# GpSimd's elementwise work put on VectorE, gather buffers lent to query reads, and two heads routed singly in a two-layer hybrid kernel

## The chip, the core and the metric

The kernel runs on one core of a Trainium2 chip. The core has a matrix engine (TensorE, PE in the profile), a vector engine (VectorE, DVE), an activation engine (ScalarE, ACT), a general engine (GpSimd, POOL) and a sequencer that only issues transfers (SyncE, SP). Each works through its own list of instructions in order; semaphores tie the lists together. The metric is the device time of one execution in microseconds (us).

## What is computed

Two layers over 256 tokens of width 1024, all in float32. The first half of a layer (called the mixer here) is an attention of 8 heads, a short convolution and two gates; the second half (the expert stage) is a product-key expert layer. Cut to what matters:

```
ada = c @ w_ada[l] + b_ada[l]                    # shift, scale, gate of both halves
h = rmsnorm(x) * (1 + sc1) + sh1
proj = h @ w_in[l]                               # q, k, v, conv and gate columns
x = x + g1 * (merged(attention, conv, gates) @ w_out[l])
h = rmsnorm(x) * (1 + sc2) + sh2
q = (h @ w_query[l]).reshape(T, 8, 2, 128)
scores = einsum("thpd,hpnd->thpn", q, sub_keys)  # 128 keys in each half of a head
top 16 of each half -> 256 sums -> top 16        # 16 experts of 16384 in each head
a = gelu(einsum("td,thkd->thk", h, expert_u[idx]))
x = x + g2 * einsum("thk,thkd->td", softmax(best) * a, expert_v[idx])
```

## The kernel before

**Mixer.** Weights come from HBM in groups of two 128x1024 tiles (1 MB), in the fixed order of a list called `stream`. `load_ahead` issues them on SP's queue as soon as one of three `raw` buffers is free. `next_unit` takes the next tile. A weight tile is split into two parts for the matmuls: ScalarE copies it to `wh` (L340), and then `wl = raw - wh` is formed (L345). Which engine forms `wl` is chosen by `l_engine`: a running sum grows by `pol["pool"]` with each tile, and a tile goes to GpSimd whenever the sum reaches one. The shares are the constants `POOL_START`, `POOL_MIX` and `POOL_PROJ` (L39), and 1.0 near the end of a mixer and of a layer. Between the weight groups lie groups of `w_ada`, which VectorE reduces: L288 multiplies a tile by the broadcast vector `cbc` and sums it up, L285 adds a scaled tile to a row. The low parts of the normalized input, `hl`, are formed at L536 and L624, partly on GpSimd.

**Query and routing.** For 16 column blocks `n`, TensorE forms queries (L940) and scores (L924). The two token tiles are `t = 1` and `t = 0`. `route` finds, for two heads of a tile at once (four key lists, `nh` is not yet a parameter), the best 16 of each list, the best 16 sums and the experts' numbers: it is a generator whose pieces `fill` places in VectorE's program between other work, up to a budget in each step.

**Experts.** Tile 0 is done densely: all 128 blocks of `expert_u` (the U stretch, L1099) and of `expert_v` (the V stretch, L1157) pass TensorE, 64 groups of 1 MB each, weighed by products of one-hot matrices that `onehots` makes (L1068 on VectorE, L1069 on GpSimd, L1071 on ScalarE). Tile 1 is done by gathers: GpSimd issues an indirect transfer for each of 128 slots (L991), 512 KB each, from `expert_u` and again from `expert_v`, into eight buffers `rows`, two in each of four `pairs`; VectorE takes them one by one (L1007, L1015) in `use`, after which the buffer goes to the next gather. `issue` issues gathers as long as a buffer is free and the heads concerned are routed.

**Lent memory.** Some tiles of the expert stage have no use yet when its reads begin, and are lent to the query and U reads: eight parts of the two activation tiles (`al`, `ah` in the profile), `hot`, and the four pairs. `place` numbers the groups of a layer: the 8 query groups are -8 to -1, the U groups 0 to 63. A lent part carries the last place for which it may be used, and `spare_part` gives a read the first part that still allows its place. Before the change all four pairs carry -5, so only one read (place -5) goes to a pair; the gathers own the pairs from the first issue on.

Of the kernel before, what the change touches and what calls it, by code (L numbers as in the profile page):

```python
# [37 lines left out]

POOL_START, POOL_MIX, POOL_PROJ = 0.5, (0.6, 0.4), 0.34  # L39


def f(ap):
    return ap.bitcast(F32)
# [3 lines left out]
def body(ctx: ExitStack, tc: tile.TileContext, d: dict, out: bass.AP):  # L47
# [469 lines left out]
    def first_norm(xps):  # L517
# [13 lines left out]
        def shift(k):  # L531
            a, b = acol[:, 0, 0, k:k + 1], adac[:, 0, 0, k:k + 1]
            z = work.tile([128, S], F32, name="hf", bufs=4)
            A.activation(hh[:, k], xh[:, k], AF.Identity, bias=b, scale=a)
            A.activation(z, xh[:, k], AF.Identity, bias=b, scale=a)
            (V if k == KD - 1 else G).tensor_tensor(hl[:, k], z, f(hh[:, k]), op=OP.subtract)  # L536

# [46 lines left out]
    def norm(l, w, kind, xps):  # L584
# [34 lines left out]
        for k in range(KD):  # L619
            while len(zs) < LEAD and k + len(zs) < KD:  # L620
                zs.append(shift(k + len(zs)))
            z, b = zs.popleft()
            if k % 2:
                G.tensor_tensor(hl[:, k], z, f(hh[:, k]), op=OP.subtract)  # L624
            else:
                V.scalar_tensor_tensor(hl[:, k], z, b, f(hh[:, k]), op0=OP.add, op1=OP.subtract)
            products(k, False)
            if k:
                products(k - 1, True)
# [19 lines left out]
    def mixer(pool, l, hh, hl, pss, vp=None):  # L649
# [157 lines left out]
        for k in range(KD - 2):  # L807
# [5 lines left out]
            tick()  # L813
        pol["pool"] = 1.0
        more["pool"] = None
# [11 lines left out]

    def route(pool, t, q, s4, sel, l, idx, whole):


        tv = pool.tile([128, 4, 16], F32, name="tv", bufs=2)
        ti = pool.tile([128, 4, 16], U32, name="ti", bufs=2)
        for i in range(4):
            while i == 2 and not whole():
                yield None
            s = s4[:, i]
            V.max(tv[:, i, 0:8], s)
            V.max_index(ti[:, i, 0:8], tv[:, i, 0:8], s)
            V.match_replace(s, tv[:, i, 0:8], s, LOW)
            V.max(tv[:, i, 8:16], s)  # L840
            V.max_index(ti[:, i, 8:16], tv[:, i, 8:16], s)
            yield 1700
        tf = pool.tile([128, 4, 16], BF, name="tf", bufs=2)
        V.tensor_copy(tf, ti)
        cand = s4.rearrange("p (n q) (a b) -> p n (q a) b", q=2, b=16)
        tvt = tv.rearrange("p (h q) k -> p h q k", q=2)
        V.tensor_tensor(cand, tvt[:, :, 0, :, None].to_broadcast([128, 2, 16, 16]),
                        tvt[:, :, 1, None, :].to_broadcast([128, 2, 16, 16]), op=OP.add)
        yield 1100
        bv = pool.tile([128, 2, 16], F32, name="bv", bufs=2)  # L850
        bp = pool.tile([128, 2, 16], U32, name="bp", bufs=2)
        for n in range(2):
            s = cand[:, n].rearrange("p a b -> p (a b)")
            V.max(bv[:, n, 0:8], s)
            V.max_index(bp[:, n, 0:8], bv[:, n, 0:8], s)
            V.match_replace(s, bv[:, n, 0:8], s, LOW)
            V.max(bv[:, n, 8:16], s)
            V.max_index(bp[:, n, 8:16], bv[:, n, 8:16], s)
            yield 2300

        cols = slice(32 * q, 32 * q + 32)
        g = sel[:, 2, cols].rearrange("p (n k) -> p n k", n=2)
        V.tensor_tensor(g, bv, bv[:, :, 0:1].to_broadcast([128, 2, 16]), op=OP.subtract)
        after(2, lambda: A.activation(g, g, AF.Exp))
        pos = pool.tile([128, 2, 32], U32, name="pos", bufs=2)
        bpf = bp.rearrange("p n k -> p (n k)")
        V.tensor_scalar(pos[:, 0], bpf, 4, None, op0=OP.logical_shift_right)
        V.tensor_scalar(pos[:, 1], bpf, 15, None, op0=OP.bitwise_and)
        posf = pool.tile([128, 2, 32], BF, name="posf", bufs=2)
        V.tensor_copy(posf, pos)  # L870
        yield 800
        tft = tf.rearrange("p (h q) k -> p h q k", q=2)
        for x in range(2):
            oh = pool.tile([128, 2, 16, 16], BF, name="oh")
            pf = posf[:, x].rearrange("p (n k) -> p n k", n=2)
            V.tensor_tensor(oh, pf[:, :, :, None].to_broadcast([128, 2, 16, 16]),
                            io16[:, None, None, :].to_broadcast([128, 2, 16, 16]), op=OP.is_equal)
            V.tensor_tensor(oh, oh, tft[:, :, x, None, :].to_broadcast([128, 2, 16, 16]), op=OP.mult)
            V.tensor_reduce(sel[:, x, cols].rearrange("p (n k) -> p n k", n=2), oh, axis=AX.X, op=OP.add)
            yield 1900  # L880
        if idx is not None:
            e = pool.tile([128, 32], F32, name="ei", bufs=2)
            V.tensor_scalar(e, sel[:, 0, cols], 128.0, float(l * 128 * NE), op0=OP.mult, op1=OP.add)
            V.tensor_tensor(e, e, sel[:, 1, cols], op=OP.add)
            V.tensor_copy(idx[:, cols], e)
            yield 400
# [69 lines left out]
    def experts(es, xp, rp, low, halves, pairs, hot, l, hf, pss):  # L956
# [69 lines left out]
        def route_all():  # L1026
            for t in (1, 0):
                for q in range(4):
                    while (t, q) not in scores:
                        yield None  # L1030
                    yield from route(rp, t, q, scores[t, q], sel[t], l, idx if t else None,
                                     lambda: (t, q) in whole)
                    if t:
                        routed.add(q)
            for _ in range(3):
# [13 lines left out]
        def step(n):  # L1049
            fill(3600 if n < 9 else 2400)  # L1050
            issue()
            if n >= 9:
                use()

        bg.append(route_all())
        query(l, hf, pss, rp, got, step)
        issue()


        def onehots(half, b):  # L1060
# [73 lines left out]
        for e in range(0, NE, 2):  # L1134
# [54 lines left out]
    for l in range(DEPTH):  # L1189
# [95 lines left out]
```

## Time and profile before

| | us |
|---|---|
| three runs, median (lowest to highest) | 1861.13 (1859.49 to 1862.21) |
| the profiled execution, its own time | 1862.17 |
| its span in the trace | 1860.4 |
| TensorE busy | 1608.0 |
| VectorE busy | 1398.7 |
| GpSimd busy | 945.4 |
| ScalarE busy | 575.4 |

The transfers moved 669.24 MB, 360 GB/s over the span. In the profile's 40 slices the rate stands between 178 and 341 GB/s in the two mixers, and between 391 and 416 GB/s in nearly all the rest. The page shows no wait of its own for the mixers: they have to be read as stretches, 0 to 248 us and 925 to 1154 us. The query block columns follow each (248 to 325, 1154 to 1232), then the U and the V stretch.

### The profile page before, as it was taken

The page shows a single profiled execution, that of the slowest core. Times are in us where ns is not written, and L with a number is a line of the kernel's source. Part 1 is how long each engine was busy: PE and PEld are TensorE (multiplying, and loading weights), DVE is VectorE, ACT ScalarE, POOL GpSimd, SP SyncE. Part 2 cuts the span into 40 slices and gives each one's busy share as a digit, 9 for nine tenths or more (in the row PEclk, how much of TensorE's full clock was granted, in tenths as well). Part 3 has the DMA queues.
Part 4 walks back from the last instruction along what each step waited for, and adds up shares of the span by engine and source line. Part 5 has one row for each costly group of instructions (what it writes and reads, how often), then busy time and mean ns, then how long its engine had stood idle before and what let it go on. Part 6 is the DMA issues. An engine that isn't in the chain of part 4 may idle for free.

```text
span 1860.4 us, 26229 instructions
## 1 busy us (share of the span) xinstructions
PE 1608.0 (86%) x9527; PEld 1260.9 (68%) x9527; DVE 1398.7 (75%) x2681; ACT 575.4 (31%) x1257; POOL 945.4 (51%) x731
## 2 busy tenths in 40 slices
PE   6799989986789989887789999998786998898776
PEld 4788878986789644532357997898785994444222
DVE  7797859999988767654565877699997887666455
ACT  3464332111166433300046443221113653431001
POOL 3435204444589777755341231244446987776551
PEclk7899999988989999999999999999898999999998
DMA  8668788999999999999945677899999999999996
GB/s 318 249 227 298 295 341 298 408 409 409 408 391 395 411 415 415 415 415 415 397 178 199 252 291 263 328 377 408 409 408 394 392 404 416 414 415 412 416 416 271
DMA packets 163203, 669.24 MB, mean 360 GB/s; under 512 B 16001, under 2 KB 16001, under 8 KB 146690
## 3 DMA queue, kind: packets, MB, share of 16 engines
q1 hardware_dynamic: 87346, 396.39, 54.3%
q0 software_dynamic: 73856, 268.48, 36.4%
q10 hardware_dynamic: 1872, 2.69, 0.4%
q8 instruction: 75, 1.23, 0.3%
q14 instruction: 54, 0.44, 0.1%
HBM read 666.46 MB, written 1.05 MB: 359 GB/s over the span
## 4 chain that ended last, share of the span: by engine, by line
DVE 31%; DMA 27%; PE 24%; issue 8%; POOL 6%; ACT 3%; SPq 0%; POOLq 0%; DVEq 0%; ACTq 0%
DMA rows<-in_expert_v_dram,idx 15%; PE mm L1099 8%; DVE rows L1007 7%; DMA raw<-in_expert_v_dram 6%; PE yp L1157 4%; POOL rows L991 4%; PE wp L1086 3%; DVE raw L288 3%; DVE y L1015 3%; DMA rows<-in_expert_rows_dram,idx 2%; DVE wl L345 2%; PE mm L394 2%; PE mm L395 1%; PE mm L396 1%; ACT wh L340 1%
## 5 line engine op out<-in xcount | busy, mean ns | idle before, releaser
L991 POOL DMA_INDIRECT rows<-in_expert_rows_dram,idx x256 | 305.6, 1194 | 335.4 <-DVE rows L1007 90.4
L991 POOL DMA_INDIRECT rows<-in_expert_v_dram,idx x256 | 329.9, 1289 | 234.2 <-DMA rows<-in_expert_v_dram,idx 97.5
L1015 DVE SCALAR_TENSOR_TENSOR y<-rows,cv,y 128x1024 f32<-128x1024 f32 x254 | 335.1, 1319 | 146.8 <-DMA rows<-in_expert_v_dram,idx 140.4
L1007 DVE SCALAR_TENSOR_TENSOR rows<-rows,h 128x1024 f32<-128x1024 f32 x256 | 328.7, 1302 | 0.4 <-DMA rows<-in_expert_rows_dram,idx 0.3
L1157 PE MATMUL yp<-raw,ah 128*128 128x512 f32 x512 | 238.9, 613 | 60.6 <-DMA raw<-in_expert_v_dram 59.4
L345 POOL TENSOR_TENSOR wl<-raw,wh 128x1024 fp32r<-128x1024 f32 x52 | 136.1, 2622 | 267.0 <-ACT wh L340 255.4
L1157 PE MATMUL yp<-raw,al 128*128 128x512 f32 x512 | 241.1, 614 | 33.8 <-DMA raw<-in_expert_v_dram 33.0
L1099 PE MATMUL mm<-hfull,raw 128*128 128x128 f32 x1984 | 239.9, 280 | 20.0 <-ACT al L1113 16.8
L1099 PEld LDWEIGHTS mm<-hfull,raw 128*128 128x128 f32 x1984 | 231.1, 195 | 20.9 <-ACT al L1113 17.2
L1071 ACT ACTIVATE hot<-iotf,iT 128x128 f32<-128x128 f32 x512 | 163.2, 390 | 263.3 <-PE wp L1086 217.5
L1157 PEld LDWEIGHTS yp<-raw,ah 128*128 128x128 f32 x512 | 94.7, 193 | 203.2 <-DMA raw<-in_expert_v_dram 103.9
L1099 PE MATMUL mm<-hfull,ah 128*128 128x128 f32 x1600 | 192.8, 282 | 13.5 <-ACT al L1113 13.5
L1099 PEld LDWEIGHTS mm<-hfull,ah 128*128 128x128 f32 x1600 | 189.3, 199 | 13.8 <-ACT al L1113 13.8
L1157 PEld LDWEIGHTS yp<-raw,al 128*128 128x128 f32 x512 | 93.8, 193 | 138.0 <-issue 96.0
L394 PE MATMUL mm<-hh,wh 128*128 128x256 f32 x512 | 149.8, 293 | 12.3 <-ACT qT L658 6.8
L340 ACT ACTIVATE wh<-raw 128x1024 fp32r<-128x1024 f32 x112 | 116.0, 1052 | 115.9 <-DMA raw<-in_w_gt_dram 47.9
L1086 PEld LDWEIGHTS wp<-hot 128*128 128x128 f32 x1024 | 129.1, 192 | 31.9 <-issue 28.5
L1069 POOL TENSOR_TENSOR hot<-hot,gT 128x256 f32<-128x256 f32 x128 | 148.6, 1161 | 2.3
L395 PE MATMUL mm<-hl,wh 128*128 128x256 f32 x512 | 146.3, 286 | 0.0
L396 PE MATMUL mm<-hh,wl 128*128 128x256 f32 x512 | 146.1, 285 | 0.0
L1086 PE MATMUL wp<-hot 128*128 128x64 f32 x1024 | 128.3, 268 | 2.8 <-POOL hot L1069 2.8
L345 DVE TENSOR_TENSOR wl<-raw,wh 128x1024 fp32r<-128x1024 f32 x60 | 92.4, 1548 | 45.4 <-ACT wh L340 45.3
(230 smaller groups left out, 2346.4 us busy)
## 6 DMA issues: line engine op xcount, KB each, us to landing
raw<-in_expert_v_dram SPq DMA_DIRECT2D x128, 1024.0 KB
raw<-in_expert_u_dram SPq DMA_DIRECT2D x62, 1024.0 KB
ah<-in_expert_u_dram SPq DMA_DIRECT2D x50, 1024.0 KB
raw<-in_w_adat_dram SPq DMA_DIRECT2D x64, 512.0 KB
raw<-in_w_gt_dram SPq DMA_DIRECT2D x16, 1024.0 KB
raw<-in_w_adag_dram SPq DMA_DIRECT2D x16, 1024.0 KB
raw<-in_w_cv_dram SPq DMA_DIRECT2D x12, 1024.0 KB
raw<-in_w_qk_dram SPq DMA_DIRECT2D x8, 1024.0 KB
```

Source lines behind the costliest of these rows:

```text
L345: l_engine().tensor_tensor(lo, raw, f(h), op=OP.subtract)
L394: T.matmul(ps, h[:, c], mh[:, k], start=first, stop=False)
L395: T.matmul(ps, h[:, c], ml[:, k], start=False, stop=False)
L396: T.matmul(ps, lo[:, c], mh[:, k], start=False, stop=last)
L991: G.indirect_dma_start(out=t, out_offset=None, in_=rows[kind], in_offset=bass.IndirectOffsetOnAxis(ap=idx[:, s:s + 1], axis=0))
L1007: V.scalar_tensor_tensor(t, t, 1.0, h1, op0=OP.mult, op1=OP.mult, accum_out=av[:, s:s + 1])
L1015: V.scalar_tensor_tensor(y1, t, cv[:, s:s + 1], y1, op0=OP.mult, op1=OP.add)
L1069: G.tensor_tensor(q, q, gT[:, ts, None].to_broadcast([128, TB, 64]), op=OP.mult)
L1071: A.activation(p[:, i], iotf, AF.Abs, bias=iT[:, b * TB + i:b * TB + i + 1])
L1086: T.matmul(ps[:, t], p[:, t], q[:, t], start=True, stop=True)
L1099: T.matmul(ps[:, u + x], raw[:, x, k * 128:(k + 1) * 128], hf[:, k, :128], start=(k == 0), stop=(k == KD - 1))
L1157: T.matmul(ys[q], halves[i // 64][:, i % 64], raw[:, x, q * 512:(q + 1) * 512], start=(i == 0), stop=(i == NE - 1))
```

## The change

Three parts. First, every elementwise instruction that GpSimd had, except three at the very end of the kernel, goes to VectorE: `wl`, `hl`, and the product in `onehots`. GpSimd keeps the gathers. Second, the four pairs carry the last places -5, -4, -3 and -2, so that they take four query reads; `free` starts empty, and `release`, called at each query step, hands a pair to the gathers once the read that was in it has been used and no later read may take it. Third, for tile 1 the first two heads are routed one after the other, each on half the lists, and `issue` looks at the head and not at the pair of heads.

```
-POOL_START, POOL_MIX, POOL_PROJ = 0.5, (0.6, 0.4), 0.34
+POOL_START, POOL_MIX, POOL_PROJ = 0.0, (0.0, 0.0), 0.0
...
-            (V if k == KD - 1 else G).tensor_tensor(hl[:, k], z, f(hh[:, k]), op=OP.subtract)
+            V.tensor_tensor(hl[:, k], z, f(hh[:, k]), op=OP.subtract)
...
-        pol["pool"] = 1.0
+        pol["pool"] = 0.0
...
-    def route(pool, t, q, s4, sel, l, idx, whole):
+    def route(pool, h0, nh, s4, sel, l, idx, whole):
...
-        for i in range(4):
+        for i in range(2 * nh):
...
-        free = deque(pair[:, i] for i in range(2) for pair in pairs)
+        free = deque()
+
+        def release():
+
+            for p in list(pairs):
+                if any(t is p for _, t in spare_of.values()):
+                    continue
+                here = [x for x in spare if x[1] is p]
+                if here:
+                    if place.get(state["dma"], 0) <= here[0][0]:
+                        continue
+                    spare.remove(here[0])
+                pairs.remove(p)
+                free.extend(p[:, i] for i in range(2))
...
-            while tasks and free and tasks[0][1] in routed:
-                assert not any(last < 0 for last, _ in spare_of.values())
+            while tasks and free and (tasks[0][1], tasks[0][2] // 16) in routed:
...
+                    for h in range(2) if t and q == 0 else [None]:
...
+                        yield from route(rp, 2 * q + (h or 0), 2 if h is None else 1, s4, sel[t], l,
+                                         idx if t else None, lambda: (t, q) in whole)
...
             fill(3600 if n < 9 else 2400)
+            release()
             issue()
...
-            G.tensor_tensor(q, q, gT[:, ts, None].to_broadcast([128, TB, 64]), op=OP.mult)
+            V.tensor_tensor(q, q, gT[:, ts, None].to_broadcast([128, TB, 64]), op=OP.mult)
...
-        for t in pairs:
-            give_back((-5, t))
+        for i, t in enumerate(pairs):
+            give_back((-5 + i, t))
```

Three places in the instruction lists show it. On VectorE, in the first layer's first norm (`wl` is the low part of a weight tile, `hl` that of the input, `raw` the tile itself):

```order
 L345 TENSOR_TENSOR wl_194<-raw_101,wh_193 128x1024
+L536 TENSOR_TENSOR hl<-hf,hh 128x256
+L345 TENSOR_TENSOR wl_205<-raw_101,wh_204 128x1024
 L345 TENSOR_TENSOR wl_215<-raw_103,wh_214 128x1024
+L345 TENSOR_TENSOR wl_222<-raw_103,wh_221 128x1024
 L288 SCALAR_TENSOR_TENSOR raw_105,adac<-raw_105,cbc 128x1024 x2
 L292 TENSOR_TENSOR adac<-adac,bcol 128x2
 L293 SCALAR_TENSOR_TENSOR acol<-adac,ngc 128x1
+L536 TENSOR_TENSOR hl<-hf,hh 128x256
```

Both halves of a weight group now stand in VectorE's list, between the reductions of `w_ada`. On SP, at the reads for the first layer's query stretch (`rows` are the pairs, `al`, `hot` and `ah` the other lent tiles):

```order
 L198 DMA raw<-in_w_query_dram 128x2x1024 x3
 L198 DMA rows_2296<-in_w_query_dram 128x2x1024
-L198 DMA al<-in_w_query_dram 128x2x1024 x4
-L198 DMA hot<-in_expert_u_dram 128x2x1024
-L198 DMA ah<-in_expert_u_dram 128x2x1024 x4
-L198 DMA raw<-in_expert_u_dram 128x2x1024 x3
+L198 DMA rows_2297<-in_w_query_dram 128x2x1024
+L198 DMA rows_2298<-in_w_query_dram 128x2x1024
+L198 DMA rows_2299<-in_w_query_dram 128x2x1024
+L198 DMA al<-in_w_query_dram 128x2x1024
 L198 DMA al<-in_expert_u_dram 128x2x1024 x3
 L198 DMA hot<-in_expert_u_dram 128x2x1024
```

Three query reads moved from `al` to the pairs, and three U reads took their place in `al`. On GpSimd, the first gathers of the changed kernel (`rows0` to `rows3` are the pairs, two buffers each):

```order
L1004 DMA rows0_2296<-in_expert_rows_dram,idx_2380 128x1024 x2
L1004 DMA rows1_2297<-in_expert_rows_dram,idx_2380 128x1024 x2
L1004 DMA rows0_2296<-in_expert_rows_dram,idx_2380 128x1024 x2
L1004 DMA rows2_2298<-in_expert_rows_dram,idx_2380 128x1024 x2
L1004 DMA rows1_2297<-in_expert_rows_dram,idx_2380 128x1024 x2
L1004 DMA rows3_2299<-in_expert_rows_dram,idx_2380 128x1024 x2
```

Before, the first eight gathers went to the four pairs in turn, twice over; now the third pair enters after six gathers and the fourth after ten.

## Rows read from the trace of the kernel before

**Rows 1.** Stretches: us, busy by engine (x instructions), PE clock, DMA share, GB/s

```profile
0.00:248.00 248.00, 208.32 (x1341) 182.35 (x1341) 198.85 (x266) 109.22 (x201) 92.57 (x53) 0.92 0.73 274
248.00:325.00 77.00, 74.61 (x413) 65.95 (x412) 56.73 (x198) 19.50 (x48) 19.35 (x18) 1.00 0.89 338
525.00:625.00 100.00, 100.00 (x898) 100.00 (x897) 84.75 (x134) 59.47 (x154) 88.99 (x71) 1.00 1.01 395
625.00:925.00 300.00, 252.68 (x748) 122.01 (x746) 183.41 (x284) 64.13 (x166) 185.78 (x148) 0.99 1.02 415
925.00:1154.00 229.00, 211.51 (x1381) 181.28 (x1382) 162.46 (x201) 105.44 (x194) 64.60 (x35) 0.96 0.63 233
```

**Rows 2.** Chain that ended last, 0 to 248 us, then 925 to 1154: shares

```profile
by line: DVE raw L288 21.2%; issue 8.3%; DVE wl L345 6.6%; ACT wh L340 5.6%; DMA raw<-in_w_cv_dram 5.0%; DMA raw<-in_w_gt_dram 4.8%; POOL wl L345 4.7%; DVE acc L285 3.9%; DMA raw<-in_w_cp_dram 2.5%; DMA raw<-in_w_out_dram 2.0%; DMA raw<-in_
...
by line: PE mm L394 10.8%; PE mm L395 9.9%; PE mm L396 9.8%; issue 6.7%; DVE wl L345 6.2%; DMA raw<-in_w_qk_dram 5.6%; ACT wh L340 4.4%; PE yp L1157 4.2%; DMA raw<-in_w_gt_dram 4.2%; DMA raw<-in_expert_v_dram 3.0%; DMA raw<-in_w_adag_dram 2
```

**Rows 3.** Lines by form, 0 to 248 us: count | busy us, mean ns | idle before

```profile
L288 DVE SCALAR_TENSOR_TENSOR raw<-raw,cbc 128x1024 f32<-128x1024 f32 x48 | 82.0, 1745 | 2.9 <-issue 1.6 <-DMA raw<-in_w_adat_dram 1.3
L345 DVE TENSOR_TENSOR wl<-raw,wh 128x1024 fp32r<-128x1024 f32 x27 | 38.3, 1422 | 20.3 <-ACT wh L340 20.2
...
L345 POOL TENSOR_TENSOR wl<-raw,wh 128x1024 fp32r<-128x1024 f32 x29 | 78.6, 2716 | 113.1 <-ACT wh L340 109.7 <-issue 3.4
```

**Rows 4.** Source lines, whole run: duration ns min/median/max, first and last start

```profile
L288 DVE SCALAR_TENSOR_TENSOR raw<-raw,cbc x64: 1210/1219/3425, 10.4 to 1060.7; 128x1024 f32<-128x1024 f32 x64
L345 DVE TENSOR_TENSOR wl<-raw,wh x60: 1207/1224/5683, 16.0 to 1144.2; 128x1024 fp32r<-128x1024 f32 x60
L1068 DVE TENSOR_TENSOR hot<-iotf,jT x128: 409/418/837, 520.5 to 1694.2; 128x256 f32<-128x256 f32 x128
```

**Rows 5.** Timeline: start us, us; a reduction on VectorE beside a subtraction on GpSimd

```profile
62.57 3.42 DVE L288 SCALAR_TENSOR_TENSOR raw<-raw,cbc 128x1024 f32<-128x1024 f32 x1
...
62.47 2.43 POOL L345 TENSOR_TENSOR wl<-raw,wh 128x1024 fp32r<-128x1024 f32 x1 [3.37 <-issue]
```

**Rows 6.** Lines by form, 925 to 1154 us; then timeline at 949 us

```profile
L345 DVE TENSOR_TENSOR wl<-raw,wh 128x1024 fp32r<-128x1024 f32 x33 | 54.1, 1652 | 25.1 <-ACT wh L340 25.1
L345 POOL TENSOR_TENSOR wl<-raw,wh 128x1024 fp32r<-128x1024 f32 x23 | 57.4, 2503 | 153.9 <-ACT wh L340 145.8 <-DVE acc L285 5.9 <-PE mm L396 2.2
...
949.50 2.26 DVE L489 SCALAR_TENSOR_TENSOR ss<-ss 128x2 f32<-128x2 f32 x1
```

**Rows 7.** Timeline of SP's queue, 247 to 335 us

```profile
247.08 0.37 SPq L198 DMA_DIRECT2D rows<-in_w_query_dram  x1
...
260.16 16.19 SPq L198 DMA_DIRECT2D raw<-in_expert_u_dram  x3
302.39 13.79 SPq L198 DMA_DIRECT2D al<-in_expert_u_dram  x3
320.63 0.37 SPq L198 DMA_DIRECT2D hot<-in_expert_u_dram  x1
324.21 11.09 SPq L198 DMA_DIRECT2D ah<-in_expert_u_dram  x4
```

**Rows 8.** Timeline: GpSimd's first gather, VectorE's first use, TensorE's query block 7

```profile
288.05 1.01 POOL L991 DMA_INDIRECT rows<-in_expert_rows_dram,idx  x1 [49.69 <-DVE sc L839]
...
293.79 1.21 DVE L1007 SCALAR_TENSOR_TENSOR rows<-rows,h 128x1024 f32<-128x1024 f32 x1
...
280.13 3.62 PE L940 MATMUL mm<-hfull,rows 128*128 128x256 f32 x16
```

**Rows 9.** Timeline of GpSimd and of VectorE in the U stretch

```profile
529.74 1.78 POOL L991 DMA_INDIRECT rows<-in_expert_rows_dram,idx  x1 [0.16 <-issue]
531.83 0.94 POOL L991 DMA_INDIRECT rows<-in_expert_rows_dram,idx  x1 [0.30 <-issue]
532.79 1.56 POOL L1069 TENSOR_TENSOR hot<-hot,gT 128x256 f32<-128x256 f32 x1
...
534.99 1.57 DVE L1007 SCALAR_TENSOR_TENSOR rows<-rows,h 128x1024 f32<-128x1024 f32 x1
```

More of the change, by code (lines that the diff above doesn't have):

```diff
@@ L623, in norm @@
             if k % 2:
-                G.tensor_tensor(hl[:, k], z, f(hh[:, k]), op=OP.subtract)
+                V.tensor_tensor(hl[:, k], z, f(hh[:, k]), op=OP.subtract)
             else:
@@ L825, in across @@
                 T.matmul(ys[2 * t + q], sl[:, ts], h[:, c], start=False, stop=last)
-    def route(pool, t, q, s4, sel, l, idx, whole):
-        tv = pool.tile([128, 4, 16], F32, name="tv", bufs=2)
-        ti = pool.tile([128, 4, 16], U32, name="ti", bufs=2)
-        for i in range(4):
+    def route(pool, h0, nh, s4, sel, l, idx, whole):
+        tv = pool.tile([128, 4, 16], F32, name="tv", bufs=2)[:, :2 * nh]
+        ti = pool.tile([128, 4, 16], U32, name="ti", bufs=2)[:, :2 * nh]
+        for i in range(2 * nh):
             while i == 2 and not whole():
@@ L842, in route @@
             yield 1700
-        tf = pool.tile([128, 4, 16], BF, name="tf", bufs=2)
+        tf = pool.tile([128, 4, 16], BF, name="tf", bufs=2)[:, :2 * nh]
         V.tensor_copy(tf, ti)
@@ L846, in route @@
         tvt = tv.rearrange("p (h q) k -> p h q k", q=2)
-        V.tensor_tensor(cand, tvt[:, :, 0, :, None].to_broadcast([128, 2, 16, 16]),
-                        tvt[:, :, 1, None, :].to_broadcast([128, 2, 16, 16]), op=OP.add)
+        V.tensor_tensor(cand, tvt[:, :, 0, :, None].to_broadcast([128, nh, 16, 16]),
+                        tvt[:, :, 1, None, :].to_broadcast([128, nh, 16, 16]), op=OP.add)
         yield 1100
-        bv = pool.tile([128, 2, 16], F32, name="bv", bufs=2)
-        bp = pool.tile([128, 2, 16], U32, name="bp", bufs=2)
-        for n in range(2):
+        bv = pool.tile([128, 2, 16], F32, name="bv", bufs=2)[:, :nh]
+        bp = pool.tile([128, 2, 16], U32, name="bp", bufs=2)[:, :nh]
+        for n in range(nh):
             s = cand[:, n].rearrange("p a b -> p (a b)")
@@ L859, in route @@
             yield 2300
-        cols = slice(32 * q, 32 * q + 32)
-        g = sel[:, 2, cols].rearrange("p (n k) -> p n k", n=2)
-        V.tensor_tensor(g, bv, bv[:, :, 0:1].to_broadcast([128, 2, 16]), op=OP.subtract)
+        cols = slice(16 * h0, 16 * h0 + 16 * nh)
+        g = sel[:, 2, cols].rearrange("p (n k) -> p n k", n=nh)
+        V.tensor_tensor(g, bv, bv[:, :, 0:1].to_broadcast([128, nh, 16]), op=OP.subtract)
         after(2, lambda: A.activation(g, g, AF.Exp))
-        pos = pool.tile([128, 2, 32], U32, name="pos", bufs=2)
+        pos = pool.tile([128, 2, 32], U32, name="pos", bufs=2)[:, :, :16 * nh]
         bpf = bp.rearrange("p n k -> p (n k)")
@@ L868, in route @@
         V.tensor_scalar(pos[:, 1], bpf, 15, None, op0=OP.bitwise_and)
-        posf = pool.tile([128, 2, 32], BF, name="posf", bufs=2)
+        posf = pool.tile([128, 2, 32], BF, name="posf", bufs=2)[:, :, :16 * nh]
         V.tensor_copy(posf, pos)
@@ L873, in route @@
         for x in range(2):
[L874 to L879, printed above, removed]
+            oh = pool.tile([128, 2, 16, 16], BF, name="oh")[:, :nh]
+            pf = posf[:, x].rearrange("p (n k) -> p n k", n=nh)
+            V.tensor_tensor(oh, pf[:, :, :, None].to_broadcast([128, nh, 16, 16]),
+                            io16[:, None, None, :].to_broadcast([128, nh, 16, 16]), op=OP.is_equal)
+            V.tensor_tensor(oh, oh, tft[:, :, x, None, :].to_broadcast([128, nh, 16, 16]), op=OP.mult)
+            V.tensor_reduce(sel[:, x, cols].rearrange("p (n k) -> p n k", n=nh), oh, axis=AX.X, op=OP.add)
             yield 1900
         if idx is not None:
-            e = pool.tile([128, 32], F32, name="ei", bufs=2)
+            e = pool.tile([128, 32], F32, name="ei", bufs=2)[:, :16 * nh]
             V.tensor_scalar(e, sel[:, 0, cols], 128.0, float(l * 128 * NE), op0=OP.mult, op1=OP.add)
@@ L1030, in route_all @@
                         yield None
[L1031 to L1034, printed above, removed]
+                    for h in range(2) if t and q == 0 else [None]:
+                        s4 = scores[t, q]
+                        if h == 1:
+                            while (t, q) not in whole:
+                                yield None
+                        s4 = s4 if h is None else s4[:, 2 * h:2 * h + 2]
+                        yield from route(rp, 2 * q + (h or 0), 2 if h is None else 1, s4, sel[t], l,
+                                         idx if t else None, lambda: (t, q) in whole)
+                        if t:
+                            routed.update([(q, 0), (q, 1)] if h is None else [(q, h)])
             for _ in range(3):
@@ L1056, in experts @@
         query(l, hf, pss, rp, got, step)
+        release()
+        assert not pairs
         issue()
@@ L1170, in experts @@
                 finish_block(1, 0)
-        pol["pool"] = 1.0
+        pol["pool"] = 0.0
         finish_block(0, 0)
```

## The prediction

> **What bounds the kernel now.** I read the profile from the outside in. First the stretches [rows 1]: in the V stretch (625 to 925 us) the transfers run at 415 GB/s, with a DMA share of 1.02. I take that as full. In the U stretch (525 to 625 us) TensorE is busy 100.00 of 100 us and the transfers still reach 395 GB/s. So these parts of the expert stage end when their bytes have arrived, or when TensorE is through. In the mixers neither holds: the first (0 to 248 us) moves 274 GB/s, the second (925 to 1154 us) 233 GB/s. Those are the stretches where an engine's order can be worth time. Between them lies the query stretch, 248 to 325 us, at 338 GB/s: against 415 a hole of (415 - 338) x 77 us = 5.9 MB, or 14 us in each layer, is open there.
>
> Next the chain of waits inside the two mixers [rows 2]. In the first, VectorE's reductions (L288) alone are 21.2% of the chain, its subtractions `wl` 6.6%, GpSimd's `wl` 4.7%, while transfers hold 5.0, 4.8, 2.5 and 2.0% and ScalarE's copies 5.6%. In the second mixer TensorE's three matmul lines hold 10.8 + 9.9 + 9.8 = 30.5%, and VectorE's `wl` 6.2%; TensorE is busy there 211.5 of 229 us.
>
> Last the durations. A reduction L288 takes 1219 ns in the median but 1745 ns on average in the first mixer, a `wl` on VectorE 1224 ns in the median and 1422 on average [rows 3, 4]. The timeline says why [rows 5]: at 62.47 us GpSimd starts a `wl` of 2.43 us, at 62.57 us VectorE starts a reduction, and it is through only after 3.42 us, 1.1 us after GpSimd's end. VectorE stood still until GpSimd was done. So GpSimd's help costs VectorE nearly what it saves it.
>
> **Part 1: the subtractions, first mixer.** Sums are made against the profiled execution's own 1862.17 us, 1.0 us above the median of the three runs. Removed: 48 x (1745 - 1219) ns = 25.2 us of standing still at L288 and 27 x (1422 - 1224) ns = 5.3 us at `wl` [rows 3, 4]. Added to VectorE: 29 `wl` x 1.224 us = 35.5 us, and 7 `hl` of 128x256 at about 0.42 us (an estimate from the equally large L1068 [rows 4]), 2.9 us. VectorE's load rises by 38.4 - 30.5 = 8 us on 198.9 of 248 [rows 1, 3]; other short instructions beside GpSimd's lose waiting too, so I take the load as unchanged. What counts is how much lies on the chain. L288 is there with 21.2% x 248 = 52.6 us of its 82.0 busy us, a share of 0.64; `wl` on VectorE with 16.4 of 38.3 us, 0.43 [rows 2, 3]. So 0.64 x 25.2 = 16.2 us and 0.43 x 5.3 = 2.3 us go, GpSimd's 4.7% x 248 = 11.7 us go, and 0.43 x 38.4 = 16.6 us come: -13.6 us. As the chain shortens, the transfers' 14.3% come nearer to being last, so I take -12. The ends: nothing of the added work on the chain, -30; all of it, 38.4 - 30.2 = +8.
>
> **Part 1, second mixer.** Removed 33 x (1652 - 1224) ns = 14.1 us, of which the chain holds 6.2% x 229 = 14.2 of 54.1 us, a share of 0.26: -3.7 us [rows 2, 4, 6]. Added 23 x 1.224 = 28.2 us, by the same share +7.3 us. At the layer boundary an instruction on two elements a partition takes 2.26 us beside GpSimd [rows 6], where next to nothing is to be computed. Several such stand in a row there, so I count about -4 us, of which the three `wl` that now stand in VectorE's list at that place take back a part. GpSimd's share of this chain is too small for its row, but the tiles it held took 2503 ns and now take 1224. I take -3 us. The ends are -17.5 (all of TensorE's idle time, 229 - 211.5) and +8.
>
> **Part 1, U stretch.** GpSimd's product (1.56 us) goes, VectorE gets 64 of 0.42 us in each layer, half of them here. A round of one weight block now holds a gather's product at 1.57 us and L1068 at up to 0.83 us [rows 4, 9]; without GpSimd beside them L1007 has 1.21 us [rows 8] and L1068 0.42 us, so the new 0.42 us is paid for by 0.36 + 0.41 us of waits that vanish. TensorE is busy throughout, so nothing is gained either: 0 us, with -5 (the 20 GB/s that are missing from 415 for 100 us are 2 MB) and +3 in each layer as ends. In the V stretch VectorE has 183 of 300 us; the cover is large.
>
> **Parts 2 and 3: the lent pairs and the single heads.** In the kernel before, SP's queue issues its batch from 247.08 us; the last U read of that batch is freed by TensorE at about 276 us, and then nothing is issued until 302.39, when three `al` parts come back from the query [rows 7]. GpSimd's first gather starts at 288.05 us [rows 8]. Afterwards three more reads of 1.05 MB (2.5 us each at 415 GB/s) go at once, so the dense batch lasts some 7.6 us longer, to about 287. But these are the very three that were issued at 302.39, and the parts now hold U groups, so the next read waits for U group 1 near 324 us (before, `hot` was ready at 320.63, freed by U group 0). Gathers: a pair is free when TensorE has passed its two query blocks. Block 7 ends at 280.13 + 3.62 = 283.75 us [rows 8], so the first two gathers start at about 284, four us earlier than now; the next pairs come two blocks later each (7.8 us), at 291.5, 299 and 307. Eight buffers are in the gathers' hands 9 us later than now (288 plus eight issues of 1.24 us are 298). By 325 us I count as many gathers as before, and one dense read less: the hole is not filled, it moves from 280-288 to 300-320. VectorE pays for the two single heads about ten more short instructions, 2 us, but does the first head in a gap that it has now. Cost +1 us in each layer, with -7.6 (the reads do fill the hole) and +4 as ends.
>
> Sum: 1862.2 - 12 - 3 + 0 + 2 = 1849 us.
>
> A row and a rule on the gathers' issue: in the U stretch an issue that starts under a VectorE instruction with two operands takes 1.78 us, one beside none 0.94 us [rows 9], so each of the 128 products put on VectorE could delay an issue by up to its 0.42 us. The Trainium skill (SBUF — State Buffer, section "Who interferes with whom") says that a tensor_tensor takes only the read side of the port pair that VectorE shares with GpSimd, and infers that descriptor writing is left alone; by that the products would cost the gathers nothing. The row speaks against the inference for this kind of instruction; the sum is the same, since GpSimd gives up 1.56 us for each, and the row only keeps rival 4 open.
>
> **Rivals.** 1. The hole is filled: both batches bring bytes in earlier that nothing gives back. For it speaks the 338 GB/s in the query stretch; against it, the order of SP's reads above. 1849 - 2 - 15 = 1832 us.
> 2. The mixers do not move: they hang on three `raw` buffers and on TensorE (208 of 248 and 211 of 229 us busy), and VectorE's waits come back elsewhere. 1862 + 2 = 1864 us, no change to be told. For it: transfers end many waits in the chain; against: the L288 pieces are the chain's largest.
> 3. Slower: VectorE becomes the one queue. Its list is in order, so a ready `wl` stands behind two or four reductions of 1.22 us, and TensorE and the `raw` buffer wait behind it, where GpSimd had taken it at once. If all added work lies on the chain: +8 in the first mixer, 28.2 + 1.7 - 7.7 = +22 in the second, 1894 us; with half of that, 1878. It decides once VectorE is busy over about 95% of a mixer's stretch. Against it: 80% now, unchanged by the sum.
> 4. The gathers' issue is starved by VectorE's 128 new products: 54 us of issue time at most, of which perhaps a third shows: 1867 us. Against it: GpSimd loses all its other work, and the transfers are full.
>
> **How the numbers follow.** Forecast 0.55, rival 1 0.13, rival 2 0.17, rival 3 0.11, rival 4 0.04. A measurement of this kernel tells 0.2%, some 3.7 us, from no change. Faster: 0.55 x 0.97 + 0.13 + a little of rival 2 = 0.69; same 0.15; slower 0.16. The range goes from 1830, rival 1's side, to 1864, rival 2's; beyond lie rivals 3 and 4 and the far end of the first mixer.
>
> **What would show it.** L288's mean at 1.22 us in the first mixer, `wl` at 1.22 us throughout; the mixers at about 236 and 226 us; the U stretch as long as before, with TensorE full; the hole in the query stretch at 300 to 320 us instead of 276 to 288, and 338 GB/s there unchanged. If the first mixer is not shorter, part 1's chain shares are wrong; if the query stretch moves clearly more than 345 GB/s, part 2 is.

## Result and the profile after

The changed kernel takes 1835.5 us (median of 4 runs, 1833.36 to 1837.66), the kernel before 1860.39 us in the same comparison (1859.49 to 1862.21): a ratio of 0.9864, with a 95% interval of 0.9851 to 0.9878. That is 25 us faster, where 13 us were forecast (1849 against the profiled execution's 1862.17). The sign and the range held; the size did not.

The stretches after, each shortened to its own length, beside [rows 1]. Columns: us, busy time of TensorE, its weight loads, VectorE, ScalarE and GpSimd (x instructions), granted clock, DMA share, GB/s:

```profile
0.00:235.30 235.30, 207.09 (x1341) 181.81 (x1341) 190.79 (x302) 110.17 (x201) 7.65 (x17) 0.93 0.78 289
525.00:625.00 100.00, 98.72 (x819) 92.76 (x818) 83.17 (x164) 60.42 (x158) 47.46 (x43) 1.00 1.01 394
625.00:913.00 288.00, 240.38 (x719) 116.60 (x717) 177.13 (x297) 58.13 (x150) 149.66 (x113) 0.99 1.02 414
913.00:1129.70 216.70, 206.69 (x1382) 178.38 (x1383) 158.14 (x228) 105.90 (x194) 1.14 (x4) 0.98 0.66 245
```

Both mixers are shorter, by about 12 us each; the U and the V stretch run as before. VectorE has 29 more `wl` in the first mixer and is still busy 8 us less there. The lines of the first mixer say why, beside [rows 3] (count | busy us, mean ns of one | idle before):

```profile
L345 DVE TENSOR_TENSOR wl<-raw,wh 128x1024 fp32r<-128x1024 f32 x56 | 67.4, 1223 | 18.3 <-ACT wh L340 18.0
L288 DVE SCALAR_TENSOR_TENSOR raw<-raw,cbc 128x1024 f32<-128x1024 f32 x48 | 56.9, 1225 | 0.0
```

A reduction takes 1225 ns instead of 1745, a subtraction 1223 instead of 1422: neither stands still any more. VectorE's 8 us are not the whole of the 12.7 us by which this mixer is shorter. In its chain of waits the reductions and `wl` of both engines held 21.2 + 6.6 + 4.7% of 248 us [rows 2], 80.6 us; afterwards they hold 14.1 + 12.0% of 235.3 us, 61.4 us, and the other pieces have grown by 6.5 us:

```profile
by line: DVE raw L288 14.1%; DVE wl L345 12.0%; PE mm L394 5.7%; ACT wh L340 5.5%; PE mm L395 4.8%; PE mm L396 4.8%; DMA raw<-in_w_cp_dram 4.8%; DMA raw<-in_w_gt_dram 4.7%; issue 3.8%; DVE acc L285 3.3%; DMA raw<-in_w_out_dram 2.6%; DMA raw
```

How much of this is VectorE's standing still, and how much GpSimd's slowness, the pair of traces does not tell apart.

To see where the time went I cut each profiled execution at three events: the first query matmul (L644) of the first layer, the first update from `yp` (L448 on VectorE, the end of the first expert stage), and the first query matmul of the second layer. All in us; the experiments below are in the same table:

| profiled execution | first mixer | first expert stage | second mixer | from there to the end |
|---|---|---|---|---|
| before | 251.0 | 689.2 | 217.4 | 702.8 |
| after | 238.2 | 689.8 | 205.3 | 702.2 |
| part 1 alone | 236.6 | 689.0 | 204.2 | 700.9 |
| parts 2 and 3 | 252.7 | 691.4 | 215.5 | 699.9 |
| parts 1 and 3 | 235.9 | 688.0 | 205.3 | 699.8 |
| GpSimd idles beside VectorE | 270.6 | 689.0 | 226.9 | 700.8 |
| 16 `wl` of the second mixer | 254.4 | 690.3 | 207.7 | 701.0 |
| before, with warm matmuls | 248.1 | 688.9 | 214.7 | 700.8 |
| parts 1 and 3, products from block 7, one a step | 235.9 | 684.8 | 205.7 | 695.9 |
| the same, two a step | 237.8 | 688.2 | 204.5 | 697.6 |
| parts 1 and 2 | 235.8 | 691.9 | 205.5 | 702.6 |
| part 3 alone | 254.4 | 685.3 | 215.9 | 700.4 |

Rows that share a stage's code show how far one trace can be trusted: the first mixer of before took 248.1 to 254.4 us, that of after 235.8 to 238.2. So the pair's 12.8 us are good to some 3 us and may rather be too small; the second mixer's 12.1 are firmer (215.5 to 217.4 against 204.2 to 205.7).

**Inside the second mixer.** Cut finer, 1.5 of the 12.1 us go at the layer boundary, 1.4 in the last value matmuls, 5.6 between the last value matmul (L581) and the first `bt` (L757), 0.3 up to the last gate, and 3.3 in the projections and the output. The 5.6 us arise at one place, read here from the timeline of the kernel before (start us, us, engine, line), with VectorE (one subtraction, then the same with the next), GpSimd, SP, ScalarE and TensorE in turn:

```profile
966.28 5.68 DVE L345 TENSOR_TENSOR wl<-raw,wh 128x1024 fp32r<-128x1024 f32 x1 [1.09 <-ACT wh L340]
...
966.28 6.82 DVE L345 TENSOR_TENSOR wl<-raw,wh 128x1024 fp32r<-128x1024 f32 x2 [1.09 <-ACT wh L340]
...
966.13 4.75 POOL L345 TENSOR_TENSOR wl<-raw,wh 128x1024 fp32r<-128x1024 f32 x2
...
973.17 0.38 SPq L198 DMA_DIRECT2D raw<-in_w_qk_dram  x1
...
981.22 1.06 ACT L340 ACTIVATE wh<-raw 128x1024 fp32r<-128x1024 f32 x1 [5.78 <-DMA raw<-in_w_qk_dram]
...
985.70 0.36 ACT L656 ACTIVATE kT<-mm 128x256 f32<-128x256 f32 x1
...
986.11 0.79 PE L678 MATMUL yp<-kT,qT 64*128 64x128 f32 x2 [3.48 <-ACT kT L656]
```

GpSimd does two subtractions in a row, and VectorE's one, begun 0.15 us later, stands through both: 5.68 us for 1.22. The `raw` tiles come free late: GpSimd's two are done at 970.88 us, VectorE's second at 973.10, and SP's next q/k read goes out at 973.17. ScalarE waits for it until 981.22, the copy of `kT` stands behind that in ScalarE's list, and TensorE waits 3.48 us for it. After the change, the same place:

```profile
950.24 5.82 DVE L345 TENSOR_TENSOR wl<-raw,wh 128x1024 fp32r<-128x1024 f32 x5 [2.93 <-ACT wh L340]
...
956.09 0.38 SPq L198 DMA_DIRECT2D raw<-in_w_qk_dram  x1
...
963.49 1.06 ACT L340 ACTIVATE wh<-raw 128x1024 fp32r<-128x1024 f32 x1 [3.09 <-DMA raw<-in_w_qk_dram]
...
968.39 0.49 PE L678 MATMUL yp<-kT,qT 64*128 64x128 f32 x2 [0.79 <-ACT kT L656]
```

Five subtractions take 5.82 us where one took 5.68. Counted from the same earlier copies on ScalarE (962.87 before, 949.15 after), the last copy starts after 14.3 us instead of 18.4. Counted so, GpSimd's two subtractions were done after 8.0 us and VectorE's second after 10.2; after the change all five are done after 6.9. The read went out 3.4 us later before the change (10.3 us after those copies, 6.9 after the change). I estimate from these times that some 2.2 us of that were VectorE's standing still and 1.1 GpSimd's own time. The clock adds to it. Windows of 3 us around the pause, before and then after (columns as above):

```profile
985.00:988.00 3.00, 1.89 (x5) 1.24 (x6) 2.58 (x7) 3.00 (x9) 0.00 (x0) 0.66 0.15 60
988.00:991.00 3.00, 3.00 (x15) 3.00 (x15) 2.97 (x4) 0.57 (x1) 2.35 (x1) 0.50 0.82 288
```

```profile
967.00:970.00 3.00, 2.21 (x15) 1.67 (x15) 2.43 (x6) 3.00 (x11) 0.00 (x0) 1.00 0.53 214
970.00:973.00 3.00, 3.00 (x26) 2.83 (x26) 2.96 (x7) 1.45 (x3) 0.00 (x0) 1.00 0.74 243
```

After the pause of 3.48 us the granted clock was 0.66 and then 0.50, the lower of its two levels (1.2 GHz). 15 matmuls went through in 3 us instead of 26; after the change the pause is 0.8 us and the clock stays at 1.00.

### The profile page after: what moved, and what is told of

Its sections match the earlier page's. It is cut to its first block, busy times and chain, and to the rows that moved or that the text cites. A ratio compares the mean times of both kernels' runs of the same rounds, so it can differ in the third digit from the quotient of the medians.

```text
span 1835.5 us, 26049 instructions
## 1 busy us (share of the span) xinstructions
PE 1603.9 (87%) x9527; PEld 1260.7 (69%) x9527; DVE 1396.4 (76%) x2902; ACT 576.4 (31%) x1259; POOL 645.1 (35%) x540
## 4 chain that ended last, share of the span: by engine, by line
DMA 34%; DVE 31%; PE 28%; ACT 3%; issue 3%; SPq 0%; POOL 0%; ACTq 0%; DVEq 0%; POOLq 0%
DMA rows<-in_expert_v_dram,idx 19%; DMA raw<-in_expert_v_dram 9%; PE mm L1121 8%; DVE rows L1020 7%; PE yp L1179 6%; PE wp L1108 4%; DVE y L1028 3%; DVE wl L345 2%; PE mm L394 2%; DMA rows<-in_expert_rows_dram,idx 2%; PE mm L395 2%; PE mm L396 2%; DVE raw L288 2%; ACT wh L340 1%; DMA raw<-in_w_gt_dram 1%
## 5 line engine op out<-in xcount | busy, mean ns | idle before, releaser
L1004 POOL DMA_INDIRECT rows<-in_expert_rows_dram,idx x256 | 299.1, 1169 | 768.3 <-ACT sc L930 436.1
L1028 DVE SCALAR_TENSOR_TENSOR y<-rows,cv,y 128x1024 f32<-128x1024 f32 x254 | 325.7, 1282 | 153.6 <-DMA rows<-in_expert_v_dram,idx 149.9
L1020 DVE SCALAR_TENSOR_TENSOR rows<-rows,h 128x1024 f32<-128x1024 f32 x256 | 306.5, 1217 | 6.2 <-DMA rows<-in_expert_rows_dram,idx 6.0
L1121 PE MATMUL mm<-hfull,ah 128*128 128x128 f32 x1600 | 187.7, 278 | 0.1
L1121 PEld LDWEIGHTS mm<-hfull,ah 128*128 128x128 f32 x1600 | 184.4, 195 | 0.5 <-ACT al L1135 0.5
L345 DVE TENSOR_TENSOR wl<-raw,wh 128x1024 fp32r<-128x1024 f32 x112 | 134.9, 1222 | 43.1 <-ACT wh L340 42.7
L394 PEld LDWEIGHTS mm<-hh,wh 128*128 128x128 f32 x512 | 99.2, 194 | 10.6 <-issue 4.3
L395 PEld LDWEIGHTS mm<-hl,wh 128*128 128x128 f32 x512 | 99.3, 194 | 0.0
```

What stands on the lines that cost most here:

```text
L345: l_engine().tensor_tensor(lo, raw, f(h), op=OP.subtract)
L394: T.matmul(ps, h[:, c], mh[:, k], start=first, stop=False)
L395: T.matmul(ps, h[:, c], ml[:, k], start=False, stop=False)
L1004: G.indirect_dma_start(out=t, out_offset=None, in_=rows[kind], in_offset=bass.IndirectOffsetOnAxis(ap=idx[:, s:s + 1], axis=0))
L1020: V.scalar_tensor_tensor(t, t, 1.0, h1, op0=OP.mult, op1=OP.mult, accum_out=av[:, s:s + 1])
L1028: V.scalar_tensor_tensor(y1, t, cv[:, s:s + 1], y1, op0=OP.mult, op1=OP.add)
```

## The experiments

The theory: the whole gain comes from part 1, in the mixers, because VectorE no longer stands still beside GpSimd; parts 2 and 3 only move the hole in the query stretch. Against it: that parts 2 and 3 carry a share, and that it was GpSimd's slowness, holding `raw` tiles, and not VectorE's standing still. All ratios are to the kernel before, with a 95% interval.

**Part 1 alone.** On the kernel before:

```diff
-POOL_START, POOL_MIX, POOL_PROJ = 0.5, (0.6, 0.4), 0.34
+POOL_START, POOL_MIX, POOL_PROJ = 0.0, (0.0, 0.0), 0.0
...
-                G.tensor_tensor(hl[:, k], z, f(hh[:, k]), op=OP.subtract)
+                V.tensor_tensor(hl[:, k], z, f(hh[:, k]), op=OP.subtract)
...
-        pol["pool"] = 1.0
+        pol["pool"] = 0.0
...
-            G.tensor_tensor(q, q, gT[:, ts, None].to_broadcast([128, TB, 64]), op=OP.mult)
+            V.tensor_tensor(q, q, gT[:, ts, None].to_broadcast([128, TB, 64]), op=OP.mult)
```

> Part 1 alone: the kernel before with every subtraction wl and hl and the one-hot product on VectorE; buffers and routing as before. Theory (the whole gain lies in the two mixers and comes from part 1): 1834 to 1840 us, with the first mixer about 236 us and the second about 217 us. Rival (the gain comes from the lent pairs and single heads, or needs them): 1849 us or more.

Measured: 1834.02 us, ratio 0.9853 (0.9836 to 0.9869), mixers 236.6 and 204.2 us by the table's cuts (the 217 us expected are counted from 913 us on, as in the stretches above, not from the first update; by that count the changed kernel has 216.7). The theory holds: part 1 carries the whole gain.

**Parts 2 and 3.** The changed kernel with the lines above turned back.

> Parts 2 and 3 alone: the changed kernel with GpSimd's subtractions and product given back to it as before. Theory (these parts only move the hole in the query stretch): 1857 to 1864 us, no change to be told, mixers 248 and 229 us long. Rival (they carry a part of the gain, or are a loss that part 1 covers): outside 1857 to 1864 us.

Measured: 1861.94 us, ratio 1.0004 (0.9992 to 1.0015). No change, as the theory had it. But beside part 1 this "nothing" is the sum of two things, as the next run shows.

**Parts 1 and 3, nothing lent beyond place -5.** The changed kernel; as before the change, one query read still goes to a pair.

```diff
         for i, t in enumerate(pairs):
-            give_back((-5 + i, t))
+            give_back((-5, t))
```

> Parts 1 and 3: the changed kernel, but all four gather pairs belong to the gathers from the start and none is lent to the query reads. Theory (bytes that come earlier in the query stretch are given back, since TensorE is full in the U stretch): 1832 to 1839 us, as the changed kernel. Rival (lending costs the gathers' early start, up to 7 us in each layer): 1822 to 1831 us.

Measured: 1828.8 us, ratio 0.9821 (0.9803 to 0.9838), the rival's range. Here the theory falls: by the medians the lending costs 6.7 us (1835.5 against 1828.8), and the single heads give 5.2 (1834.02 to 1828.8). The intervals leave each of these sizes open by some 4 us, and the traces put less of them where they belong: between the changed kernel and this run the two expert stages differ by 1.8 and 2.4 us, between part 1 alone and this run by 1.0 and 1.1. GpSimd's gathers in the changed kernel and in this run (start us, us, idle before and its releaser):

```profile
268.03 1.01 POOL L1004 DMA_INDIRECT rows<-in_expert_rows_dram,idx  x1 [203.15 <-ACT sc L930]
271.24 1.00 POOL L1004 DMA_INDIRECT rows<-in_expert_rows_dram,idx  x1 [2.19 <-PE mm L940]
275.13 0.94 POOL L1004 DMA_INDIRECT rows<-in_expert_rows_dram,idx  x1 [2.89 <-PE mm L940]
279.03 0.94 POOL L1004 DMA_INDIRECT rows<-in_expert_rows_dram,idx  x1 [2.96 <-PE mm L940]
```

```profile
260.97 1.01 POOL L1004 DMA_INDIRECT rows<-in_expert_rows_dram,idx  x1 [196.07 <-PE mm L940]
262.29 0.96 POOL L1004 DMA_INDIRECT rows<-in_expert_rows_dram,idx  x1 [0.30 <-issue]
263.55 0.94 POOL L1004 DMA_INDIRECT rows<-in_expert_rows_dram,idx  x1 [0.30 <-issue]
264.80 0.94 POOL L1004 DMA_INDIRECT rows<-in_expert_rows_dram,idx  x1 [0.31 <-issue]
```

Without lending the gathers start as soon as the first head is routed. Lent pairs come back a query block or two apart (the waits on `mm` L940), so the first gather waits until 268 us, and the eighth follows 19 us after it and not 10. Over 90 us, beginning 3 us ahead of each trace's own first query matmul, the transfers run at 349 GB/s in the changed kernel and at 359 without lending (the third line is for a later comparison):

```profile
235.20:325.20 90.00, 88.13 (x537) 79.81 (x536) 73.25 (x247) 23.28 (x54) 26.21 (x25) 1.00 0.93 349
...
232.90:322.90 90.00, 88.12 (x537) 79.85 (x536) 73.25 (x247) 23.34 (x54) 26.22 (x25) 1.00 0.94 359
422.90:522.90 100.00, 71.78 (x575) 71.16 (x575) 88.11 (x191) 22.63 (x49) 48.38 (x42) 0.85 1.02 403
```

**GpSimd idles beside VectorE.** The changed kernel, in which GpSimd again subtracts at the places of before, but a constant from itself into a tile that nobody reads. Nothing waits for it, and it waits for no weight tile, so these subtractions run in bursts (seven in a row from 72.48 us).

```diff
-POOL_START, POOL_MIX, POOL_PROJ = 0.0, (0.0, 0.0), 0.0
+POOL_START, POOL_MIX, POOL_PROJ = 0.5, (0.6, 0.4), 0.34
...
-        l_engine().tensor_tensor(lo, raw, f(h), op=OP.subtract)
+        if l_engine() is G:
+            ...
+                idle = src.tile([128, D], BF, name="idle")
+                G.tensor_tensor(idle, cbc, cbc, op=OP.subtract)
+        V.tensor_tensor(lo, raw, f(h), op=OP.subtract)
...
-        pol["pool"] = 0.0
+        pol["pool"] = 1.0
```

> The changed kernel, and GpSimd does subtractions again at the places where it did them in the kernel before: 29 in the first mixer, 20 in the second, each from a constant into a tile that nobody reads. So GpSimd takes its port time from VectorE, but no raw tile waits for it. Theory (VectorE's standing still beside GpSimd is the cost): a reduction L288 takes 1.6 us or more on average in the first mixer, and the time is 1844 to 1862 us. Rival (what counted was that GpSimd is slow and holds the raw tiles): 1834 to 1841 us, although reductions take longer.

Measured: 1892.95 us, ratio 1.0168 (1.0149 to 1.0186), slower than before and outside both ranges. L288 takes 1563 ns on average (the theory said 1600 or more). The lines of the first 268 us, and the share line of its chain:

```profile
L350 DVE TENSOR_TENSOR wl<-raw,wh 128x1024 fp32r<-128x1024 f32 x56 | 79.5, 1441 | 12.9 <-ACT wh L340 12.7
L288 DVE SCALAR_TENSOR_TENSOR raw<-raw,cbc 128x1024 f32<-128x1024 f32 x48 | 73.2, 1563 | 0.0
L349 POOL TENSOR_TENSOR idle<-cbc 128x1024 bf16<-128x1024 f32 x29 | 72.6, 2504 | 8.0 <-DVE cbc L244 5.9
```

```profile
by line: DVE raw L288 21.7%; DVE wl L350 20.6%; issue 8.7%; DMA raw<-in_w_cp_dram 4.3%; DMA raw<-in_w_gt_dram 4.1%; ACT wh L340 4.1%; DVE acc L285 3.3%; DMA raw<-in_w_adag_dram 2.3%; DMA raw<-in_w_out_dram 1.8%; DMA xt<-in_x_dram 1.8%; DVE 
```

Standing still: 48 x (1563 - 1220) + 56 x (1441 - 1224) ns = 28.6 us (the medians of both lines from this trace), and the first mixer is 270.6 - 238.2 = 32.4 us longer. With all of `wl` on VectorE, a us of standing still came out as about a us of the mixer; other short instructions' waits come on top. The rival falls as it was put: GpSimd held nothing, and the time rose. That GpSimd's slowness cost nothing beside it in the kernel before is not shown; no run takes away the one and keeps the other. The size was missed because I priced the waits by their share of the chain, 0.4 to 0.6, once more. In the second mixer these subtractions come in one burst at its start (961.6 to 1002.6 us), so its 21.6 us don't compare with before place by place.

**16 `wl` of the second mixer.** On the kernel before; the other seven there, and the first mixer, stay:

```diff
-POOL_START, POOL_MIX, POOL_PROJ = 0.5, (0.6, 0.4), 0.34
+POOL_START, POOL_MIX, POOL_PROJ = 0.5, (0.6, 0.0), 0.34
```

> The kernel before, with 16 of the second mixer's 23 subtractions wl (those from q/k to gates) on VectorE; its boundary, its projections and the first mixer as before. Theory (three wl in a row on VectorE that stand still beside GpSimd's hold the raw tiles and delay the q/k read; the rest follows from that): the second mixer is 8 to 10 us shorter (207 to 209 us from the first update on yp to the first query matmul, before 217.4), TensorE's pause ahead of L678 under 1 us, time 1850 to 1854 us. Rival (the prediction's share of the chain, 3 us for all of part 1 there): 1857 to 1861 us.

Measured: 1852.47 us, ratio 0.9964 (0.9951 to 0.9977); second mixer 207.7 us, TensorE's pause 0.47 us:

```profile
986.32 0.48 PE L678 MATMUL yp<-kT,qT 64*128 64x128 f32 x2 [0.47 <-ACT kT L656]
```

One constant gives 9.7 of the 12.1 us of this mixer, as the theory had it. The stretch from L581 to L757 takes 32.7 us (before 38.7, after 33.1), so 6.0 of the 9.7 us arise there. The run takes away VectorE's standing still and GpSimd's slowness together.

**Warm matmuls in the pause.** On the kernel before, eight matmuls ahead of the third head's scores:

```diff
+            if l and n == 2:
+                keep_warm(8)
             ps = y_ps([128, 384])
```

> The kernel before, with eight matmuls of a constant (128x512) put in front of the third head's scores in the second mixer, which nobody reads, so that TensorE is not idle during its pause of 3.5 us. Theory (about half of the 5.6 us of that stretch is the granted clock that falls after the pause): clock 1.00 from 980 to 1000 us, second mixer 214 to 215.5 us, time 1857 to 1860 us. Rival (the clock is a sign of the pause, and costs nothing of its own): 217 us or more, 1860 to 1863 us.

Measured: the granted clock is 1.00 all through, the stretch takes 35.4 us instead of 38.7, the second mixer 214.7:

```profile
982.00:985.00 3.00, 2.30 (x16) 1.97 (x17) 2.54 (x7) 2.99 (x9) 0.00 (x0) 1.00 0.20 53
985.00:988.00 3.00, 3.00 (x23) 2.50 (x22) 3.00 (x3) 1.57 (x5) 2.38 (x1) 1.00 0.82 322
```

1.45 us of pause are left behind the eight matmuls (3.48 before). So about 3 of the 5.6 us are the slow clock behind the pause, and 2 to 3 the pause itself. The whole time, 1858.04 us, ratio 0.9992 (0.9977 to 1.0007), can't show so little; this rests on the trace.

**More bytes earlier.** On parts 1 and 3, the products of gathered rows begin at block 7 instead of 9, with one in each step, and with two:

```diff
-            if n >= 9:
+            if n >= 7:
                 use()
+                use()
```

> Parts 1 and 3 without lending, and the products of the gathered rows begin at the seventh query block instead of the ninth, so the gather buffers come free two blocks (7.8 us) earlier. Theory (the buffers' return sets the bytes of the query stretch from 270 us on): more than 363 GB/s from 235 to 325 us, and 1824 to 1828 us. Rival (VectorE is full there, so what it does earlier it misses later): 1827 to 1831 us.

> As the run before, with two products in each step from the seventh block on instead of one from the ninth. Theory (VectorE's routing is ahead of need, products are not): 370 GB/s or more from 235 to 325 us, and 1818 to 1826 us. Rival (routing comes late and the scores' tiles with it): TensorE waits in the query stretch, and 1829 us or more.

Measured: 1828.69 us (0.9814 to 0.9853) and 1829.22 us (0.9799 to 0.9846), no different from 1828.8 (the first one's trace is of its fastest execution, 1824.09 us). The bytes did come earlier, and were nearly given back, as the windows of the second run show, counted as above:

```profile
234.80:324.80 90.00, 88.13 (x537) 79.89 (x537) 72.24 (x236) 21.45 (x51) 35.87 (x30) 1.00 0.99 382
424.80:524.80 100.00, 69.03 (x520) 68.42 (x521) 91.38 (x204) 16.78 (x31) 53.90 (x44) 0.80 0.99 385
```

23 GB/s more for 90 us are 2.1 MB; 18 GB/s less for 100 us, from 190 us after the window's start on, are 1.8 MB. The rival had TensorE waiting in the query stretch; it did not wait there (88.13 of 90 us busy, 88.12 without the edit), and the theory's time was wrong too.

**Parts 1 and 2, and part 3 alone.**

> Parts 1 and 2: the changed kernel, with the first two heads of tile 1 routed together as before. Theory (lending costs only because it keeps the pairs from gathers that are already routed; routed together, they are ready about 274 us, when two pairs are back): 1832 to 1837 us, as part 1 alone (1834.0). Rival (lending costs its 6.7 us whenever it is there): 1838 to 1843 us.

> Part 3 alone: the kernel before with the first two heads of tile 1 routed singly; subtractions, product and pairs as before. Theory (gathers that start some 13 us earlier are worth 5 us, whatever the mixers do): 1853 to 1857 us. Rival (the gain needs GpSimd free of other work): 1858 to 1863 us.

Measured: parts 1 and 2 1836.22 us, ratio 0.9879 (0.9856 to 0.9902); part 3 alone 1858.69 us, ratio 0.9997 (0.9985 to 1.001). The first is in the theory's range: with heads routed in pairs the first gather starts at 272.85 us, when lending has little left to hold back. By the medians it costs about 2 us beside part 1 alone, but the interval reaches to 1842 us, into the rival's range, so this run does not decide between them.

The second is in the rival's range, but not for the rival's reason. The first gather starts 25.2 us after the first query matmul, as in parts 1 and 3 (25.1), and not 37 as before. Counted as above, the query stretch carries 361 GB/s with GpSimd's other work in place, where the kernel before has 348:

```profile
248.00:338.00 90.00, 87.61 (x530) 78.95 (x529) 69.40 (x229) 22.89 (x52) 25.40 (x23) 1.00 0.91 348
...
251.40:341.40 90.00, 88.13 (x537) 79.80 (x536) 73.17 (x247) 23.29 (x54) 26.46 (x25) 1.00 0.95 361
```

In this one trace the expert stages are 3.9 and 2.4 us shorter than before's, and the first mixer, whose code is the same, is 3.4 us longer, within its scatter. The interval allows a gain of at most 2.8 us. So the bytes come earlier with or without part 1; whether the single heads are worth more beside part 1 than alone stays open.

No version measured is clearly faster than parts 1 and 3, 1828.8 us.

## Why the prediction was half the size

- **First mixer, -12.** Measured 12.8 less in the pair of traces, 10 to 19 over all traces of either code. The durations held: L288 at 1225 ns (1220 forecast), the mixer at 235.3 us (236). That the number agrees is in part luck: the pieces of the chain that the sum goes over fell by 19.2 us, not by 13.6, and other pieces took 6.5 of that back; the same way of pricing failed in the second mixer and in the run with idle subtractions.
- **Second mixer, -3: the step that failed.** It is 12.1 us shorter. I multiplied 14.1 us of standing still by `wl`'s share of the chain, 0.26, and set the added `wl` at the same share. Both were wrong in kind. Its written terms, -3.7 + 7.3 - 4, come to -0.4; the -3 leaned on GpSimd's faster tiles, which had no working. The chain of before [rows 2] puts 5.6% of 229 us, 12.8 us, on the q/k reads; the sum leaves these alone, as if they were the transfers' own, but the reads were late because VectorE and GpSimd held `raw` (5.68 us for one `wl`, above). After the change they hold 3.4% of 216.7 us, 7.4 (the line below). And the added `wl` cost far less than the share's 7.3 us: VectorE, at 162.5 of 229 us, took 23 of them and was busy 4 us less in all. I had seen [rows 6] that its mean was 1652 ns, not that the excess comes in clusters ahead of the q/k units. The slow clock behind the pause, some 3 us, was not in the sum at all: its far end, -17.5, was TensorE's idle time with its busy time kept, but over the whole mixer the busy time fell too, from 211.5 to 206.7 us for the same matmuls, and the idle time from 17.5 to 10.0. What moved the mixer is shown by the run with 16 `wl`: 9.7 us.

```profile
by line: PE mm L394 11.8%; PE mm L395 11.1%; PE mm L396 11.0%; DVE wl L345 8.0%; ACT wh L340 5.1%; DMA raw<-in_w_gt_dram 5.0%; issue 4.7%; PE yp L1179 4.5%; DMA raw<-in_w_qk_dram 3.4%; DMA raw<-in_expert_v_dram 3.3%; DVE acc L285 2.3%; DMA 
```

- **Second mixer's boundary, -4.** 1.5 us between the first update and L508; the rest of the gain lies further on.
- **U stretch, 0.** The first expert stage went from 689.2 to 689.8 us. Rival 4 fell: the gathers' issues in the U stretch (525 to 625 us) take 937 ns in the median, before 978, with the longest 1.86 us, before 1.91. The Trainium skill (SBUF — State Buffer, section "Who interferes with whom") leads to no cost there, and the trace agrees on the sum. The 1.78 us of [rows 9] stood beside L1015 (527.84 to 530.67 us), a SCALAR_TENSOR_TENSOR, which is another kind of instruction than the products (TENSOR_TENSOR).
- **Parts 2 and 3, +1 us in each layer.** Measured +0.6 and -0.6 us; beside part 1 alone the two parts cost 1.5 us by the medians, less than the intervals tell. The hole moved as described (331 GB/s from 275 to 300 us, 285 from 300 to 325). The lump was right, the content not: I priced the heads at 2 us of VectorE's time, while by the medians they give 5.2 us beside part 1, and lending at next to nothing, while it costs 6.7.
- **The rivals.** The hole was not filled (349 GB/s over the 90 us counted above, before 348), so rival 1 fell, although its 1832 us lay nearest; VectorE is busy 81% of the first mixer, so rival 3's point was never reached.

Term by term: 1862.2 - 12.8 - 12.1 + 0.6 - 0.6 = 1837.3 us; the changed kernel's profiled execution took 1837.62 us.

## What to carry to other kernels

Where two engines take turns at standing still, the share of the chain is a poor price, even if it comes out right once: the excess comes in clusters, and a late buffer shows up in the chain as a slow transfer and a pause of TensorE. Look at the longest single instance (5.68 us for 1.22) and follow who is late behind it, clock included. Take a bundle of edits that adds up to nothing apart, since one part can be paying for another. And when two traces are compared by windows, count them from the same event in each: in the run with part 3 alone the 90 us from 248 us on read 345 GB/s, which hides the gain, and those from 251.4 us on read 361.

## What the runs showed of the hardware

- One VectorE subtraction stood through two GpSimd subtractions in a row (5.68 us); in the run with idle subtractions, while GpSimd did seven in 19.85 us, VectorE's instructions took 2.90 us each, one after the other.
- That GpSimd read a constant and wrote bf16, 2504 ns each, did not spare VectorE its waits: 28.6 us beside 29 of them, against 30.5 us beside 29 `wl` of before.
- A TensorE pause of 3.48 us was followed by 0.66 and 0.50 of the full clock in the next 3-us windows; with eight matmuls in it, 1.45 us of pause were left and the clock stayed at 1.00.
